# Loading the first two blocks of x as halves over two DMA queues, with the identity between them, and one sum of squares moved to VectorE

## The chip, the cores and the metric

The kernel runs on one core of one Trainium2 chip. A core has five engines with an instruction stream each: PE (TensorE, matrix products), ACT (ScalarE), DVE (VectorE), POOL (GpSimd) and SP (SyncE). SP and ACT each issue DMA transfers on a queue of their own: the profile calls SP's queue q1 and ACT's q10. The metric is the time of one execution on the device in microseconds. Before the change, three executions took 1043.51, 1043.86 and 1046.29 us; their median is 1043.86 us.

## What is computed

A decoder layer on 512 tokens of width 1024: a root-mean-square norm, one wide projection, three mixers, a gated merge, a feed-forward block and a last norm. The change touches the first lines only:

```python
def rmsnorm(x, g):
    xf = x.astype(jnp.float32)
    y = xf * lax.rsqrt(jnp.mean(xf * xf, axis=-1, keepdims=True) + NORM_EPS)
    return (y * g.astype(jnp.float32)).astype(x.dtype)
...
    for i in range(DEPTH):
        u = rmsnorm(x, ln1_g[i])
        proj = u @ w_in[i]
```

All that follows (attention, pooling, state-space scan, feed-forward) reads `proj`, so nothing of it can begin before the first tokens are normed and turned.

## The kernel before, in words

The 512 tokens are four blocks of 128. A block is loaded as two tiles of 128 x 512 floats (256 KB each): `xin[tb, 0]` and `xin[tb, 1]`, the left and the right half of the features. `load_x` (L1410 to L1413) issues the two transfers of one block. Before the change, block 0 goes out on SP's queue and block 1 on ACT's; then ACT's queue takes the 128 x 128 identity `eye` (L1418) and the norm's gains `g8` (L1419). SP's queue goes on with the first weight tile in two halves of 512 KB (`fetch(weights[0], 2)`, L179), the second of 1 MB, then blocks 2 and 3 of x and small tables.

ACT then loads a table (L1422), and PE runs `warm_up` (L1427), products of ones that no result depends on.

The opening loop (`for tb in range(2)`, around L1488 to L1500) takes blocks 0 and 1. For each it sums squares of both halves (`squares`: ACT at L432, DVE at L434; the accumulated sum is read by a short second instruction), forms the mean square `v` (L1492, L1493) and its root `sq` on ACT (L1494), refines the reciprocal on DVE (`r`, `rt`, L1495 to L1497), and multiplies the identity by it into a diagonal tile `diag[tb]` (L1498). A product of a block of x with `diag[tb]` turns the block and scales it at once: `turn_scale` (L1486), eight for a block, 16 PE instructions in the profile. The eight of block 0 are issued inside the loop, right behind `diag[0]`. Behind the loop PE turns `g8` (L1502, with the identity), then takes the eight of block 1.

On ACT, behind the loop, stand two casts of the first weight tile (`wh`, L191), then the eight evacuations `turned` (L1456, high part `uh`, with the low part `ul` on DVE at L1457), then two casts of the second weight tile, sums of squares for blocks 2 and 3 (`row_squares`), and their scaling (L1523 on ACT, L1521 on DVE). POOL forms the low part of the first weight tile (L211). PE goes on with `begin` (L1469): 80 instructions on the first 256 tokens, then the transposes of the scaled blocks 2 and 3 (L1534), then the rest.

The order on PE, ACT, DVE and POOL is that of the program text (`manual_schedule` over these four engines); SP follows the order in which its transfers are asked for. An engine executes in order: an instruction that waits holds back all behind it.

Of the kernel before, what the change touches and what calls it, by code (L numbers as in the profile page):

```python
# [16 lines left out]
P = 128  # L17
S = 512
# [65 lines left out]
def trunk(ctx: ExitStack, tc, out, x, rel_bias, ln1_g, w_in, b_gate, w_a, pool_w, pool_scale, w_b,  # L84
# [3 lines left out]
    act, dve, pool, pe, sp = nc.scalar, nc.vector, nc.gpsimd, nc.tensor, nc.sync  # L88

    x, w_in, w_a, w_b, w_c, w_o = x[0], w_in[0], w_a[0], w_b[0], w_c[0], w_o[0]  # L90
# [17 lines left out]
    def T(name, dt=F32, shape=(P, S)):  # L108
        return big.tile(list(shape), dt, name=name, tag="t")
# [7 lines left out]
    def small(name, shape, dt=F32):  # L117
        return tiny.tile(list(shape), dt, name=name, tag="tiny")
# [310 lines left out]
    def squares(eng, src, ss):  # L429
        junk = T("junk")  # L430
        if eng is act:
            act.activation(junk, src, AF.Square, accum_out=ss)  # L432
        else:
            dve.scalar_tensor_tensor(junk, src, 1.0, src, OP.mult, OP.mult, accum_out=ss)  # L434
# [972 lines left out]

    xin, warm = {}, small("warm", [P, 1])

    def load_x(tb, eng=sp):  # L1410
        for h in range(2):
            t = xin[tb, h] = T("xin")
            eng.dma_start(t, x[tb * P:(tb + 1) * P, h * S:(h + 1) * S])  # L1413

    g8, g1 = T("g8"), cpool.tile([P, KD], F32, name="g1")
    load_x(0)
    load_x(1, act)
    act.dma_start(eye, c_eye)  # L1418
    act.dma_start(g8[:KD, :P], ln1_g[0].rearrange("(k p) -> k p", p=P))  # L1419
    dve.memset(ones, 1.0)  # L1420
    dve.memset(warm, 1.0)
# [7 lines left out]
    fetch(weights[0], 2)  # L1429
    fetch(weights[1])  # L1430
    load_x(2)
    load_x(3)
    sp.dma_start(ramp, c_ramp.partition_broadcast(P))
# [51 lines left out]
    def turn_scale(tb, k):  # L1485
        pe.matmul(bank(k)[:, tb * P:(tb + 1) * P], x_block(tb, k), diag[tb][:, :P], start=True, stop=True)  # L1486

    for tb in range(2):  # L1488
        s0, s1, v, sq, r, rt = (small(n, [P, 1]) for n in ("s0", "s1", "v", "sq", "r", "rt"))
        squares(act, xin[tb, 0], s0)  # L1490
        squares((dve, act)[tb], xin[tb, 1], s1)
        dve.tensor_scalar(v, s0, 1.0 / D, EPS, OP.mult, OP.add)  # L1492
        dve.scalar_tensor_tensor(v, s1, 1.0 / D, v, OP.mult, OP.add)  # L1493
        act.activation(sq, v, AF.Sqrt)  # L1494
        dve.reciprocal(r, sq)  # L1495
        dve.scalar_tensor_tensor(rt, r, v, r, OP.mult, OP.mult)
        dve.tensor_scalar(rt, rt, -0.5, 1.5, OP.mult, OP.add)  # L1497
        dve.tensor_scalar(diag[tb][:, :P], eye, r, rt, OP.mult, OP.mult)  # L1498
        if tb == 0:
            for k in range(KD):  # L1500
                turn_scale(0, k)
# [15 lines left out]
    for tb in (2, 3):  # L1517
        for h in range(2):
            t = xin[tb, h]
# [98 lines left out]
```

## Time and profile before

| what | value |
|---|---|
| three executions, median | 1043.86 us |
| the profiled execution's own time | 1044.67 us |
| its span (first to last instruction in the records) | 1042.3 us |
| mean granted PE clock | 0.997 |
| PE busy | 1030.8 us |
| DVE busy | 689.9 us |
| ACT busy | 483.7 us |
| POOL busy | 136.1 us |
| bytes moved by DMA | 115.51 MB |

The profiled execution took 1044.67 us, 2.37 us more than its span, and 0.81 us more than the median of the three. In the views below, a row of the timeline gives its start, its length, engine, line and operation, and in brackets what the engine waited for; `x8` says that eight instructions are merged into the row. A row with `SPq` or `ACTq` is the issue of a transfer by that engine, not the transfer. A row of the chain of waits gives start, length, and what the program's end hung on in that stretch. A row of the stages gives each engine's busy time, then the granted clock of PE, the share of the DMA engines and GB/s. A row of the DMA queues gives packets, MB, and the packets' time as a share of 16 engines.

### The profile page before, as it was taken

What the parts mean: (1) busy time and instruction counts of PE and PEld (TensorE: products, weight loads), DVE (VectorE), ACT (ScalarE), POOL (GpSimd) and SP (SyncE); (2) the same over time, 40 slices, a digit from 0 to 9 for tenths busy, and PEclk for the clock granted to TensorE, in tenths of its full rate; (3) what the DMA queues carried; (4) which work ended last, traced back from release to release, by engine and by line L of the source; (5) the groups of instructions that cost most, each with busy time, mean ns of one, the idle gap of its engine ahead of it and who ended that gap; (6) DMA issues with size and microseconds to landing.
All of it is one profiled execution on the core that took longest, in us unless ns stands there. A gap on an engine that the chain in (4) does not pass through costs nothing.

```text
span 1042.3 us, 13073 instructions
## 1 busy us (share of the span) xinstructions
PE 1030.8 (99%) x5196; PEld 859.8 (82%) x5196; DVE 689.9 (66%) x924; ACT 483.7 (46%) x779; POOL 136.1 (13%) x118
## 2 busy tenths in 40 slices
PE   8999999999999999999999999999999999999997
PEld 8988877898888887787887888898888888888885
DVE  4563565774356647576568855767778769876776
ACT  5432445443474263566554333544445544454332
POOL 1680000000000001100134500001111000111002
PEclk9999999999999999999999999999999999999999
DMA  8445222027222354541243535443222232412222
GB/s 268 132 111 153 91 72 75 31 56 205 83 81 81 81 154 109 152 123 50 81 139 106 196 118 202 165 141 120 83 93 70 81 122 83 160 41 81 81 81 81
DMA packets 116427, 115.51 MB, mean 111 GB/s; under 512 B 5235, under 2 KB 101302, under 8 KB 116367
## 3 DMA queue, kind: packets, MB, share of 16 engines
q1 hardware_dynamic: 115775, 113.83, 35.8%
q8 instruction: 41, 0.67, 0.3%
q10 hardware_dynamic: 592, 0.86, 0.2%
q14 instruction: 19, 0.16, 0.0%
HBM read 110.87 MB, written 2.22 MB: 109 GB/s over the span
## 4 chain that ended last, share of the span: by engine, by line
PE 94%; DVE 3%; DMA 1%; ACT 1%; issue 1%; POOL 0%; ACTq 0%; DVEq 0%; POOLq 0%
PE pa L230 32%; PE pu L230 22%; PE pb L230 12%; PE pqk L230 9%; PE pd L230 7%; PE pa L1469 2%; PE ps L656 1%; PE pu L1279 1%; PE po L695 1%; PE pt L683 1%; PE ppw L230 1%; PE py L955 1%; DVE wl L211 1%; PE pyo L961 1%; DMA wb<-wd 1%; DMA eye<-in_c_eye_dram 1%
## 5 line engine op out<-in xcount | busy, mean ns | idle before, releaser
L211 DVE TENSOR_TENSOR wl<-raw,wh 128x2048 fp32r<-128x2048 f32 (+3 forms) x92 | 214.5, 2332 | 52.1 <-ACT wh L191 43.9
L191 ACT CAST wh<-raw 128x1024 fp32r<-128x1024 f32 (+3 forms) x182 | 183.6, 1026 | 42.4 <-DMA raw<-in_w_in_dram 15.2
L230 PE MATMUL pa<-uh,wh 128*128 128x512 f32 x384 | 98.7, 399 | 0.0
L1152 DVE SCALAR_TENSOR_TENSOR hc<-pu,fcol,hc 128x510 f32<-128x510 f32 x88 | 65.9, 748 | 48.8 <-ACT hc L1149 47.2
L230 PE MATMUL pa<-uh,wl 128*128 128x512 f32 x384 | 95.0, 389 | 0.8 <-DVE wl L211 0.8
L230 PE MATMUL pa<-ul,wh 128*128 128x512 f32 x384 | 95.0, 389 | 0.0
L230 PEld LDWEIGHTS pa<-uh,wl 128*128 128x128 f32 x384 | 72.0, 188 | 16.2 <-DVE wl L211 1.3
L230 PEld LDWEIGHTS pa<-ul,wh 128*128 128x128 f32 x384 | 72.1, 188 | 15.2
L230 PE MATMUL pu<-uh,wh 128*128 128x512 f32 (+1 forms) x352 | 83.6, 379 | 0.0
L230 PE MATMUL pu<-ul,wh 128*128 128x512 f32 (+1 forms) x352 | 83.5, 379 | 0.0
L230 PE MATMUL pu<-uh,wl 128*128 128x512 f32 (+1 forms) x352 | 83.5, 379 | 0.0
L230 PEld LDWEIGHTS pa<-uh,wh 128*128 128x128 f32 x384 | 70.2, 188 | 15.3 <-issue 1.0
L230 PEld LDWEIGHTS pu<-ul,wh 128*128 128x128 f32 x352 | 64.2, 188 | 12.5
L230 PEld LDWEIGHTS pu<-uh,wl 128*128 128x128 f32 x352 | 64.2, 188 | 12.5
L230 PEld LDWEIGHTS pu<-uh,wh 128*128 128x128 f32 x352 | 64.1, 188 | 12.4
L1157 POOL TENSOR_TENSOR hc<-hc 128x512 f32<-128x512 f32 x22 | 31.7, 1441 | 288.4 <-DVE hc L1152 253.6
L1149 ACT ACTIVATE hc<-pu,fcol,fcol 128x512 f32<-128x512 f32 x40 | 31.2, 779 | 80.5 <-PE pu L230 80.5
L934 POOL TENSOR_TENSOR xd<-xc,dec 128x512 f32<-128x512 f32 x6 | 6.4, 1063 | 360.0 <-DVE xc L925 334.3
L677 ACT ACTIVATE sb<-sb,nm 128x128 f32<-128x128 f32 (+1 forms) x72 | 30.1, 419 | 24.1 <-DVE nm L674 17.2
L1050 ACT ACTIVATE sg<-pa,col 128x512 f32<-128x512 f32 x24 | 16.5, 687 | 50.8 <-PE pa L230 50.7
L230 PE MATMUL pqk<-uh,wh 128*128 128x512 f32 x144 | 36.9, 393 | 0.0
L230 PE MATMUL pqk<-ul,wh 128*128 128x512 f32 x144 | 36.3, 389 | 0.0
(347 smaller groups left out, 1818.1 us busy)
## 6 DMA issues: line engine op xcount, KB each, us to landing
raw<-in_w_in_dram SPq DMA_DIRECT2D x25, 1024.0 KB
raw<-in_ffn_w_up_dram SPq DMA_DIRECT2D x22, 1024.0 KB
raw<-in_w_in_dram SPq DMA_DIRECT2D x20, 512.0 KB
raw<-in_w_o_dram SPq DMA_DIRECT2D x8, 1024.0 KB
raw<-in_ffn_w_down_dram SPq DMA_DIRECT2D x6, 1024.0 KB
raw<-in_w_b_dram SPq DMA_DIRECT2D x4, 1024.0 KB
al<-ad SPq DMA_DIRECT2D x16, 256.0 KB
w<-in_ffn_w_down_dram SPq DMA_DIRECT2D x4, 1024.0 KB
```

The lines of the kernel that those rows point to most:

```text
L191: act.copy(job.high[:, :, o], job.raw[:, :, o])
L211: (eng or dve).tensor_tensor(l[:, :, o], job.raw[:, :, o], h[:, :, o].bitcast(F32), OP.subtract)
L230: pe.matmul(ps, l, r, start=first and n == 0, stop=last and n == total - 1)
L656: pe.matmul(pss[i][:, o:o + w * P], q[r, n * P:(n + 1) * P], k[r, kb * P:(kb + w) * P], start=True, stop=True)
L677: act.activation(sb[:, off:off + w * P], sb[:, off:off + w * P], AF.Exp, bias=nm[:, n, h:h + 1], accum_out=ls[:, n, h:h + 1])
L683: pe.transpose(pt[:, o:o + P], sb[:, o:o + P], eye)
L695: pe.matmul(po[DH * hh:DH * hh + DH, n * P:(n + 1) * P], V[g, kb + i][:, (2 * c + hh) * DH:(2 * c + hh + 1) * DH], probs[2 * c + hh, nb][: ...
L1050: act.activation(s, ps, AF.Sigmoid, bias=col[:, o:o + 1])
L1149: act.activation(t, ps, AF.Identity, bias=ff["c1"][:, ff["b"] + m:ff["b"] + m + 1], scale=fw(2, m))
L1152: dve.scalar_tensor_tensor(t[:, sh:], ps[:, :S - sh], fw(k, m), t[:, sh:], OP.mult, OP.add)
L1157: pool.tensor_tensor(a, a, t, OP.mult)
L1469: pe.matmul(first[2 * n + j][:, lo:hi], a[:, k, j * P:(j + 1) * P], b[:, k, lo:hi], start=a is wh and b is uh and k == 0, stop=a is wl and ...
```

## The change

Three edits, all in the opening. `load_x` takes a pair of queues, one for each half. The two halves of block 0 go out on SP's and ACT's queue, so do the halves of block 1, and the identity stands between them on ACT's queue. The squares of the right half of block 1 are summed on DVE, where ACT did it.

The order on the two queues is:

| | SP's queue | ACT's queue |
|---|---|---|
| before | block 0 left, block 0 right, weights 0 ... | block 1 left, block 1 right, identity, `g8` |
| after | block 0 left, block 1 left, weights 0 ... | block 0 right, identity, block 1 right, `g8` |

```diff
@@ -1407,15 +1407,15 @@
-    def load_x(tb, eng=sp):
+    def load_x(tb, engs=(sp, sp)):
         for h in range(2):
             t = xin[tb, h] = T("xin")
-            eng.dma_start(t, x[tb * P:(tb + 1) * P, h * S:(h + 1) * S])
+            engs[h].dma_start(t, x[tb * P:(tb + 1) * P, h * S:(h + 1) * S])
 
     g8, g1 = T("g8"), cpool.tile([P, KD], F32, name="g1")
-    load_x(0)
-    load_x(1, act)
+    load_x(0, (sp, act))
     act.dma_start(eye, c_eye)
+    load_x(1, (sp, act))
     act.dma_start(g8[:KD, :P], ln1_g[0].rearrange("(k p) -> k p", p=P))
@@ -1488,7 +1488,7 @@
     for tb in range(2):
         s0, s1, v, sq, r, rt = (small(n, [P, 1]) for n in ("s0", "s1", "v", "sq", "r", "rt"))
         squares(act, xin[tb, 0], s0)
-        squares((dve, act)[tb], xin[tb, 1], s1)
+        squares(dve, xin[tb, 1], s1)
         dve.tensor_scalar(v, s0, 1.0 / D, EPS, OP.mult, OP.add)
```

## The prediction

> **What bounds the kernel now.** I read the page's chain of waits first, then the same chain in order of time, then the timeline of the opening.
>
> ```profile
> span 1042.3 us, 13073 instructions
> PE 94%; DVE 3%; DMA 1%; ACT 1%; issue 1%; POOL 0%; ACTq 0%; DVEq 0%; POOLq 0%
> ```
>
> ```profile
> 1.66 6.35 DMA eye<-in_c_eye_dram
> 8.11 0.34 DVE diag L1498
> 8.53 2.85 PE uT L1486 x16
> 11.38 0.20 PE pa L1502
> 11.59 2.66 PE uT L1486 x16
> 14.24 9.60 PE pa L1469 x80
> 23.84 1.75 PE uT L1534 x16
> ```
>
> The kernel is PE from end to end, except that the chain begins with the identity's transfer. What the change can win is therefore the start of PE's useful work and its pace up to the first long run of products. The identity, third on ACT's queue, lands at 1.66 + 6.35 = 8.01 us, and the first `diag` follows at 8.11. The identity alone is late by little, as the timeline shows:
>
> ```profile
> 0.74 0.89 ACTq L1413 DMA_DIRECT2D xin<-in_x_dram  x2
> 0.74 0.87 SPq L1413 DMA_DIRECT2D xin<-in_x_dram  x2
> 1.05 5.35 PE L1427 MATMUL pa<-ones 128*128 128x128 f32 x24 [1.05 <-DVE relb L511]
> ...
> 4.73 0.63 ACT L432 ACTIVATE junk<-xin 128x512 f32<-128x512 f32 x1 [0.34 <-DMA xin<-in_x_dram]
> 5.26 0.19 ACT L432 ACTIVATION_READ_ACCUMULATOR junk<-xin 128x1 f32 x1
> 5.70 0.69 DVE L434 SCALAR_TENSOR_TENSOR junk<-xin 128x512 f32<-128x512 f32 x1 [4.67 <-DMA xin<-in_x_dram]
> ...
> 6.32 0.15 DVE L1492 TENSOR_SCALAR v<-s 128x1 f32<-128x1 f32 x1
> 6.69 0.20 ACT L1494 ACTIVATE sq<-v 128x1 f32<-128x1 f32 x1 [1.24 <-DVE v L1493]
> 6.80 0.61 ACT L432 ACTIVATE junk<-xin 128x512 f32<-128x512 f32 x1
> 7.38 0.15 DVE L1497 TENSOR_SCALAR rt<-rt 128x1 f32<-128x1 f32 x1
> 7.41 0.61 ACT L432 ACTIVATE junk<-xin 128x512 f32<-128x512 f32 x1
> 8.11 0.34 DVE L1498 TENSOR_SCALAR diag<-eye,r,rt 128x128 f32<-128x128 f32 x1 [0.58 <-DMA eye<-in_c_eye_dram]
> 8.82 0.20 ACT L1494 ACTIVATE sq<-v 128x1 f32<-128x1 f32 x1 [0.70 <-DVE v L1493]
> 8.93 2.09 ACT L191 CAST wh<-raw 128x1024 fp32r<-128x1024 f32 x2
> 9.70 0.35 DVE L1498 TENSOR_SCALAR diag<-eye,r,rt 128x128 f32<-128x128 f32 x1
> 12.78 3.44 ACT L1456 ACTIVATE uh<-uT,g 128x256 fp32r<-128x256 f32 x8 [1.76 <-PE uT L1486]
> ```
>
> The scale of block 0 is ready at 7.38 + 0.15 = 7.53, so 0.58 us of DVE's wait is the identity's. Behind it stands a second late transfer: the right half of block 0, for which DVE waits until 5.70, while ACT began the left half at 4.73. And PE stands still from the warm-up's end (6.40) to 8.51, for which it pays twice:
>
> ```profile
> 6.40:8.51 2.11, 0.00 (x1) 0.00 (x0) 1.16 (x7) 1.43 (x5) 0.00 (x0) 1.00 1.21 295
> ...
> 9.50:13.00 3.50, 3.50 (x18) 3.25 (x17) 0.67 (x3) 1.73 (x3) 2.96 (x2) 0.51 1.08 355
> ```
>
> For the 3.50 us that begin 1.0 us after the gap the granted clock is 0.51: 3.50 x 0.49 = 1.7 us of PE work lost, in the turns of blocks 0 and 1. The two groups of turns with `g8` between them take 8.53 to 14.24 = 5.71 us; at full clock they would take 4.0, about 1.9 a group and 0.2 for `g8`.
>
> **The change part by part.** ACT issues four transfers before its table load in both kernels, and SP two ahead of the weights; the issue rows keep their count and place, so the issuing itself costs nothing new. What moves is which bytes stand ahead of which.
>
> *Block 0.* The queues' packets tell when each transfer ran.
>
> ```profile
> q1 hardware_dynamic: 150, 0.28, 50.0%
> q10 hardware_dynamic: 137, 0.25, 34.7%
> ```
>
> ```profile
> DMA packets 272, 0.47 MB, mean 315 GB/s; under 512 B 23, under 2 KB 47, under 8 KB 272
> ```
>
> From 1.75 to 3.75 us (first pair of rows) each queue moved one half block of 0.26 MB side by side. ACT's first place now holds block 0's right half, so it should land with the left one, near 4.7. From 3.75 to 5.25 (third row) 0.47 MB went at 315 GB/s.
>
> DVE then sums from 4.75 on, until 4.75 + 0.69 = 5.44. ACT's sum of the left half is read at 5.26 + 0.19 = 5.45, and this becomes the bound: `v` at about 5.5 instead of 6.32. From `v` to the scale's end takes 7.53 - 6.32 = 1.21, so the scale is ready at 6.7. The identity, now second on ACT's queue, runs beside block 1's left half: 0.07 + 0.26 = 0.33 MB at 315 GB/s is 1.05 us from 3.75, so its last packet falls by 4.8. How long from the last packet to the landing, the identity of before tells:
>
> ```profile
> q10 hardware_dynamic: 197, 0.13, 20.5%
> ...
> q10 hardware_dynamic: 2, 0.00, 0.1%
> ```
>
> In 5.25 to 7.25 ACT's queue still moved 197 packets, after 7.25 two; the landing is at 8.01, so 0.76 later. The identity then lands near 5.6, over 1 us before it is needed. `diag[0]` starts at 6.75 and PE at 7.15 instead of 8.51: 1.36 us earlier. PE's gap shrinks from 2.11 to 0.75 us.
>
> *The clock.* The trace shows no gap of 0.75 us at the start, so this is bounded: with the half-clock stretch gone 1.7 us come on top, with the stretch as before nothing. I take it as gone, being nearer to the long busy stretches at 1.00 than to a gap of 2.11. Every other wait of PE until 14.24 then counts as well.
>
> The Trainium skill (TensorE: Matmul & The Clock Gate, Why this matters for your kernels) says that the clock falls for PE gaps longer than about 3 us. The row above disagrees: 2.11 us were followed by 0.51. By the page the gap did not cause the stretch, and the change would leave it; that is the first of the rivals.
>
> *Block 1.* The left half, on SP's queue by 4.8, lands near 5.6; ACT squares it behind its root of block 0, at about 6.0. The cost is in the right half, third on ACT's queue and beside the first weights on SP's. How ACT's queue fares against those weights, the identity of before shows, from 5.75 to 7.0:
>
> ```profile
> q1 hardware_dynamic: 692, 0.35, 101.2%
> q10 hardware_dynamic: 129, 0.06, 16.4%
> ```
>
> One packet of ACT's against 5.4 of the weights', in 1.25 us. The right half is 128 packets of 2 KB: by packets it takes 128 x (2 KB + 5.4 x 0.5 KB) = 0.62 MB at (0.35 + 0.06) MB / 1.25 us = 1.9 us, from about 4.8, so it ends at 6.7 and lands at 7.5. The bounds: one packet against one weight packet, 0.33 MB or 1.0 us, landing at 6.6; or the same bytes a microsecond as the identity, 0.06 / 1.25, 5.4 us, landing at 11.0. The row is nearer to packets, since two streams of equal packets did not share equally there by bytes either; I take 7.5.
>
> DVE is free at 6.75 + 0.34 = 7.1 and so waits 0.4 us for it; behind it on DVE stand only block 1's chain and the copy of the gains. From this sum's start to the scale's end took 5.70 to 7.53 = 1.83 for block 0, so `diag[1]` starts at 9.35 (before: 9.70) and PE's second group at 9.75. PE finishes its first group at 7.15 + 1.9 = 9.05 and `g8` at 9.3: 0.45 us idle. The second group ends at 11.7, against 14.24: 2.5 us.
>
> *What ACT does with it.* ACT loses one sum (0.61 + 0.19 for reading). Its root of block 1 comes at 7.5 + (6.69 - 5.70) = 8.5 instead of 8.82, so the first cast could start at 8.6. The second cast needs the second half of the first weights:
>
> ```profile
> q1 hardware_dynamic: 2066, 1.06, 102.5%
> ```
>
> From 5.0 to 9.0 SP's queue moved 1.06 MB, which is this tile of 1.05 MB; landing at 9.0 + 0.76 = 9.75. The bytes ahead of it are the same in both kernels. So the second cast runs from 9.75 to 10.8 (2.09 / 2 each) instead of ending at 11.02, and `turned` starts at 10.85, instead of 12.78 behind PE's slow turns: ACT and all behind it on ACT is 1.9 us earlier, PE 2.5. What is late next is the scaling of blocks 2 and 3, of which ACT's part ended at 22.12 + 1.34 = 23.46 and PE's first weight load of them began at 23.57:
>
> ```profile
> 22.12 1.34 ACT L1523 ACTIVATE xin<-xin,r 128x512 f32<-128x512 f32 x2 [1.08 <-DVE r L426]
> ...
> 23.57 0.46 PEld L1534 LDWEIGHTS uT<-eye,xin 128*128 128x128 f32 x4
> ```
>
> 0.1 us of slack. PE, 2.5 us early, meets scaled blocks that are 1.9 us early and waits the 0.5 us between: **the sum is 1.9 + 0.1 = 2.0 us**, less 0.1 for small waits: 1.9. After that the chain is PE, and where it leaves PE it starts from PE's progress, so the shift carries to the end: 1044.67 - 1.9 = 1042.8 for the profiled execution, and by the median, 0.81 lower, **1042.0**.
>
> **The rivals.** *The clock stretch stays* (or the timed executions of before did not have it). PE's second group then runs from 9.75 at half clock until 13.0 and the rest at full: 1.6 us of its 1.9 are done by then, it ends at 13.3, and 14.24 - 13.3 = 0.9 us is left: 1043.86 - 0.9 = 1043.0 (this and the next times go from the median). For it: there is still a gap in the same place, and one more of 0.45. Against it: together they are 1.2 us, not 2.11. The clock page of the Trainium skill (TensorE: Matmul & The Clock Gate) is on this rival's side, as said above.
>
> *Only the identity counts.* If block 0's right half is no sooner on the other queue, the scale stays at 7.53 and only the wait of 0.58 goes; with the stretch at half clock as before the gain is 0.6: 1043.3. For it: the two queues together moved 315 GB/s already, so a second queue adds no rate. Against it: half as many bytes stand ahead of that half as before. The Trainium skill (DMA: Bandwidth & Descriptors, Rules for kernel authors) says that spreading DMAs over issuing engines brings no bandwidth and only saves issue time; the rows above agree as to the rate, and by that rule alone the time would be this rival's 1043.3; the forecast goes by the order of the bytes instead.
>
> *The right half of block 1 starves, and the kernel is slower.* On ACT's queue beside the weights it may get bytes as the identity did, landing at 11.0. ACT's second cast ends 0.99 + 2.2 = 3.2 us behind the start of DVE's sum; `turned` is later than 12.78 once the half lands after 9.5. At 11.0 it starts at 14.25: 1.5 us lost, and PE, idle from 9.3 to 13.3, falls to half clock again and loses up to 1.7 more: 1.5 to 3.2 us, 1045.4 to 1047.1. For it: ACT's queue moved only 0.06 MB in 1.25 us there. Against it: equal packets in number, not in bytes, explain that as well.
>
> *The order does not reach the queues*, or the shift is lost in a later wait: 1043.9. Against it: the transfers are issued in program order in the rows above.
>
> **How the numbers follow.** The forecast (1.5 to 2.3 us gained) has 0.52, the clock stretch staying 0.20, the identity alone 0.08, starvation 0.12, no effect 0.08. The forecast's own range is 1041.5 to 1042.4; the executions of before spread over 2.8 us, so a median moves by some 0.7 us by itself. The range for the time is 1040.7 to 1044.4: it takes in the first two rivals and no effect, and leaves out most of starvation. A change of under 0.3% (3.1 us) can hardly be told from none here. To be faster by that, the time must be under 1040.7, which the sum reaches only with luck in the median: 0.10. Slower by that needs the worst of starvation: 0.05. The rest, 0.85, is no change.
>
> **What would show it.** In the profile after: DVE's first sum of squares near 4.7 and not 5.7; `diag[0]` near 6.75 with no wait for the identity; PE's turns from 7.15 with the granted clock at 1.00 until 14; DVE waiting for block 1's right half until about 7.5; the casts of the first weights ending at 10.8; `turned` at 10.85; the products of L1469 from 11.7; and a short wait of PE at L1534, near 21.6, for ACT's scaling. A landing of block 1's right half after 9.5 makes the prediction wrong in sign, a half-clock stretch behind 9.5 halves it.

## The result, and the profile after

The changed kernel took 1042.30 us in the median of 22 executions (1041.21 to 1043.84), the kernel before 1043.68 us in 22 executions beside them (1041.24 to 1046.29). The ratio is 0.9987 with a 95% interval of 0.9981 to 0.9993: 1.4 us or 0.13% faster. The interval leaves out 1, and the gain is well inside the 0.3% that the prediction named as the bound of "no change". The forecast was 1042.0 us. One profiled execution in the experiments (the first set with the longer warm-up) took 1475.71 us at a mean granted clock of 0.65; it is left out, and that kernel was profiled again.

The changed kernel's page and its chain of waits in order of time (start, length, what the end hung on):

```profile
span 1038.6 us, 13072 instructions
PE 97%; DMA 1%; DVE 1%; ACT 0%; issue 0%; ACTq 0%; DVEq 0%; SPq 0%
```

```profile
1.66 5.62 DMA xin<-in_x_dram
7.31 0.70 DVE junk L434 x2
...
9.18 0.36 DVE diag L1498
9.54 0.04 issue
9.58 2.05 PE uT L1486 x16
11.63 9.68 PE pa L1469 x80
21.31 1.75 PE uT L1534 x16
```

The chain no longer begins with the identity but with a half block of x, block 1's right one, and goes through its sum and `diag[1]` to PE's second group of turns. The run of 80 products starts at 11.63 instead of 14.24, the turns of blocks 2 and 3 at 21.31 instead of 23.84: the opening is 2.5 us shorter in this pair of profiles. The same stretch in the timeline of the changed kernel (start, length, engine, line, and what the engine waited for):

```profile
4.61 0.63 ACT L432 ACTIVATE junk<-xin 128x512 f32<-128x512 f32 x1 [0.23 <-DMA xin<-in_x_dram]
4.79 0.69 DVE L434 SCALAR_TENSOR_TENSOR junk<-xin 128x512 f32<-128x512 f32 x1 [3.76 <-DMA xin<-in_x_dram]
...
6.66 0.34 DVE L1498 TENSOR_SCALAR diag<-eye,r,rt 128x128 f32<-128x128 f32 x1
...
7.06 2.05 PE L1486 MATMUL uT<-diag,xin 128*128 128x128 f32 x16 [1.50 <-DVE diag L1498]
7.31 0.69 DVE L434 SCALAR_TENSOR_TENSOR junk<-xin 128x512 f32<-128x512 f32 x1 [0.30 <-DMA xin<-in_x_dram]
...
9.85 1.04 ACT L191 CAST wh<-raw 128x1024 fp32r<-128x1024 f32 x1 [0.41 <-DMA raw<-in_w_in_dram]
...
10.80 3.02 ACT L1456 ACTIVATE uh<-uT,g 128x256 fp32r<-128x256 f32 x8
```

Block 0's right half is there at 4.79, not at 5.70; `diag[0]` follows at 6.66 with no wait for the identity. PE's turns start at 7.06, after a gap of 1.50 us and not of 2.11. And the clock holds. In this row of the stages the column before the last two is the granted clock:

```profile
9.50:13.00 3.50, 3.42 (x29) 3.40 (x30) 1.79 (x7) 3.15 (x8) 3.48 (x2) 1.00 1.08 356
```

The same 3.50 us had 0.51 before and 18 PE products where there are 29 now. How much of the gain that is, and whether it was the transfers that brought it, the experiments tell.

### The profile page after: what moved, and what is told of

It is laid out like the page before. It is cut to its first block, busy times and chain, and to the rows that moved or that the text cites. A ratio compares the mean times of both kernels' runs of the same rounds, so it can differ in the third digit from the quotient of the medians.

```text
span 1038.6 us, 13072 instructions
## 1 busy us (share of the span) xinstructions
PE 1028.1 (99%) x5196; PEld 857.8 (83%) x5196; DVE 689.4 (66%) x926; ACT 482.9 (46%) x777; POOL 135.8 (13%) x118
## 4 chain that ended last, share of the span: by engine, by line
PE 97%; DMA 1%; DVE 1%; ACT 0%; issue 0%; ACTq 0%; DVEq 0%; SPq 0%
PE pa L230 36%; PE pu L230 22%; PE pb L230 12%; PE pqk L230 9%; PE pd L230 7%; PE pa L1469 2%; PE ps L656 1%; PE pu L1279 1%; PE po L695 1%; PE pt L683 1%; PE ppw L230 1%; DMA al<-ad 1%; PE py L955 1%; DMA xin<-in_x_dram 1%; PE pyo L961 1%; PE pst L972 0%
## 5 line engine op out<-in xcount | busy, mean ns | idle before, releaser
L627 DVE COPY k<-pqk 128x512 f32<-128x512 f32 x9 | 6.2, 690 | 45.3 <-PE pqk L230 45.3
```

## The experiments

There were three sets, each timed beside the kernel before in five rounds on one chip. The first holds "before again", "sum on DVE alone", "identity first, alone" and "two queues alone"; the second "changed again", "changed, warm-up 17", "right half on SP" and "before, warm-up 20"; the third the rest. The kernel before had medians of 1043.84, 1043.15 and 1043.76 us in them. Ratios are to that kernel, with 95% intervals. They are not quotients of the medians: "changed, identity third" has 1042.44 against 1043.76 us, a quotient of 0.9987, and a ratio of 0.9993. "Gap" is PE's longest wait before a group of turns, "half clock" whether the profile shows a granted clock of 0.5 in the opening, "start" the start of the run of 80 products. These three and the span come from one profiled execution each.

| kernel | median us | ratio (interval) | gap us | half clock | start us | span us |
|---|---|---|---|---|---|---|
| before (as shown ahead) | 1043.68 | 1 | 2.1 | yes | 14.24 | 1042.3 |
| before again | 1043.75 | 0.9993 (0.9985 to 1.0002) | 2.6 | yes | 14.10 | 1041.5 |
| sum on DVE alone | 1044.10 | 1.0000 (0.9991 to 1.0008) | 2.2 | yes | 14.20 | 1041.8 |
| identity first, alone | 1042.39 | 0.9990 (0.9981 to 0.9999) | 1.5 | no | 12.69 | 1040.7 |
| two queues alone | 1042.01 | 0.9981 (0.9972 to 0.9989) | 0.9 | no | 11.88 | 1039.2 |
| changed | 1042.30 | 0.9987 (0.9981 to 0.9993) | 1.5 | no | 11.63 | 1038.6 |
| changed again | 1042.23 | 0.9988 (0.9979 to 0.9998) | 1.5 | no | 12.66 | 1040.6 |
| changed, warm-up 17 | 1042.45 | 0.9989 (0.9981 to 0.9998) | 0.6 | no | 11.82 | 1039.6 |
| changed, warm-up 6 | 1042.43 | 0.9993 (0.9984 to 1.0003) | 2.9 | yes | 12.73 | 1039.7 |
| changed, identity third | 1042.44 | 0.9993 (0.9983 to 1.0002) | 1.7 | no | 12.42 | 1039.9 |
| right half on SP | 1041.58 | 0.9986 (0.9977 to 0.9995) | 1.2 | no | 11.54 | 1039.0 |
| right half on SP, warm-up 17 | 1042.46 | 0.9994 (0.9985 to 1.0004) | none | no | 11.44 | 1039.7 |
| before, warm-up 20 | 1041.47 | 0.9981 (0.9971 to 0.9990) | - | - | - | - |
| before, warm-up 20, again | 1041.54 | 0.9984 (0.9975 to 0.9993) | 1.1 | no | 12.57 | 1039.7 |

**The kernel before, again.** No edit.

> The kernel before, unchanged. Theory (the clock is a matter of where its windows fall): the times spread over some 4 us as in the 22 runs (1041.2 to 1046.3) around 1043.7, ratio 1.000, and the profile may show the half-clock stretch behind 9.5 us at another place or not at all; the DVE and ACT stall near 530 to 568 us need not be there. Rival (both belong to the kernel): half clock from 9.5 to 13.0 and the chain off PE from 528 to 568 again.

The chain of waits and a row of the stages of this execution:

```profile
14.10 9.59 PE pa L1469 x80
```

```profile
8.40:11.70 3.30, 3.30 (x16) 3.30 (x16) 1.04 (x5) 2.18 (x3) 1.80 (x1) 0.51 1.12 332
```

Half the theory held. The half-clock stretch came at another place (8.4 to 11.7), so its position moves, but the profile showed it again, and again in the kernel with the sum alone. In all three profiles with the old transfers and the old warm-up it is there. The chain did not leave PE near 530 to 568 us this time, as the theory allowed.

The record has the mean granted clock of every execution, and this accounts for much of the spread of the times. A stretch of 3.4 us at half clock takes 0.0016 off that mean (3.4 x 0.5 / 1042), and half clock at the program's end (from 1040.37 us on in the first profile of the kernel before) takes another 0.001 to 0.002 off. So 0.997 or less is a sign of the stretch in the opening. It is not a proof: the profiled execution of the sum alone has the stretch and reads 0.998. The kernel before, sorted by this reading:

| set | at 0.998 or 0.999 | their median us | at 0.997 or less | their median us |
|---|---|---|---|---|
| first | 4 | 1042.28 | 29 | 1044.06 |
| second | 12 | 1042.34 | 21 | 1043.88 |
| third | 12 | 1041.50 | 23 | 1044.10 |

In the third set the two groups do not even touch: 1040.8 to 1042.3 us and 1043.5 to 1045.5. All 33 executions of the changed kernel read 0.998 or 0.999. In the second set it took 1042.23 us, about what the executions of the kernel before took that kept their clock (1042.34). As far as times can tell, then, most of the gain of the change is that the stretch no longer occurs.

**The two queues alone.** Block 1's right half is summed on ACT, as before.

```diff
-        squares(dve, xin[tb, 1], s1)
+        squares((dve, act)[tb], xin[tb, 1], s1)
```

> The two queues alone, block 1's right half summed on ACT again. Theory: the order of the bytes makes the gain and the move of the sum next to none, since the second cast waits for the weights' second half (9.85) in any case: DVE's first sum at 4.8, PE's turns from 7.1, second group 0.1 to 0.2 us later than in the changed kernel, products from 11.6 to 11.8; time 1042.3 to 1042.5. Rival (the sum on DVE is needed): ACT, with 0.8 us more in front of the casts, is late and the gain over before falls to half, 1043.0.

```profile
7.61 0.63 ACT L432 ACTIVATE junk<-xin 128x512 f32<-128x512 f32 x1 [1.17 <-DMA xin<-in_x_dram]
...
8.66 2.16 ACT L191 CAST wh<-raw 128x1024 fp32r<-128x1024 f32 x2
```

1042.01 us, a little under the expected range, with DVE's first sum at 4.62, turns from 6.90 and products from 11.88. The theory held in its direction: the move of the sum is worth nothing that can be seen here. Its reason did not hold: the two casts follow each other (2.16 us for both), with no wait for weights worth naming. ACT had stood idle for 1.17 us when the right half landed, so the sum cost nothing there, and the chain goes, as in the changed kernel, from that landing through the sum and `diag[1]` to PE's second group.

**The sum on DVE alone.**

```diff
-        squares((dve, act)[tb], xin[tb, 1], s1)
+        squares(dve, xin[tb, 1], s1)
```

> The sum on DVE alone, queues as before. Theory: no gain; DVE takes the sum up behind diag[0] (8.45), diag[1] comes at about 10.4 instead of 9.7, the casts end at 11.5 instead of 11.0; 0 to 0.4 us slower than before where PE is at full clock, nothing where it is at half clock: 1043.7 to 1044.1. Rival: it makes part of the gain, 1043.0 or less.

The ratio is 1.0000 (0.9991 to 1.0008), the median 1044.10 us; `diag[1]` started at 10.20 instead of 9.70. As the theory expected, no gain.

**The identity first, alone.** Both halves of block 0 on SP's queue, both of block 1 on ACT's, the identity ahead of them.

```diff
     load_x(0)
+    act.dma_start(eye, c_eye)
     load_x(1, act)
-    act.dma_start(eye, c_eye)
```

> The identity first on ACT's queue, ahead of block 1, block 0 on SP's queue as before. Theory: only DVE's wait of 0.58 us goes, diag[0] at 7.55 and PE's turns from 7.95; gain 0.4 to 0.9 us: 1042.8 to 1043.3. Rival (the identity was all that counted): the whole gain, 1042.3, with the turns from 7.1.

1042.39 us, with a ratio (0.9990) that cannot be told from the changed kernel's (0.9987). Who waited for whom on PE (total, times, longest), a row of the stages, and the chain:

```profile
PE uT L1486 <- DVE v L1492: 1.5, 1, 1.5
```

```profile
8.10:13.00 4.90, 4.52 (x37) 4.31 (x38) 2.21 (x9) 4.36 (x9) 2.42 (x2) 1.00 1.12 337
```

```profile
12.69 9.59 PE pa L1469 x80
```

Mechanically the theory was right: only DVE's wait went, and the turns started at 8.05, 0.46 us earlier than before. But in this execution that shortened the gap from 2.1 to 1.5 us (0.14 of it because the warm-up ended at 6.54 and not at 6.40), and the clock stayed at 1.00. The run of 80 starts 1.5 us earlier, not 0.5: the size came from the clock, and neither side of the expectation had that.

The clock did not stay in every execution. Five of the 11 read 0.996 or 0.997, with a median of 1043.04 us; the other six, the profiled one among them, have 1041.93. So the identity's place alone keeps the clock only at times, where the changed kernel kept it in all 33.

**The kernel before with a longer warm-up**, in two sets. Every transfer and every instruction of the opening is as before; PE multiplies ones until 7.3 us.

```diff
-WARM = 12
+WARM = 20
```

> The kernel before with 20 products of warm-up instead of 12, so that PE is busy until about 8.4. Theory (the gap of 2.1 us lets the clock fall): no half-clock stretch, the turns of block 0 still from 8.5 at full clock, products from 12.5 to 13.0 instead of 14.2; the times' spread shrinks to about that of the changed kernel (1041.2 to 1043.8) and the median falls by 0.5 to 1.0: 1042.7 to 1043.2. Rival (the stretch has nothing to do with the gap): the same spread and 1043.7 or slightly more.

> The kernel before with 20 products of warm-up, a second time, for a profile at an undisturbed clock. Theory (the change's gain is for the most part the clock, which falls in a gap of 2.1 us or more): turns of block 0 from about 8.5, full clock throughout, first products' run of 80 from 12.7 to 12.9, time 1041.3 to 1041.8, as good as the changed kernel or better with none of its edits. Rival (its time came from something later): half clock in the opening, or a start of the 80 at 14, and the gain behind it.

1041.47 and 1041.54 us, ratios of 0.9981 and 0.9984. The second set's waits, stages and chain:

```profile
PE uT L1486 <- DVE v L1492: 1.1, 1, 1.1
```

```profile
8.40:13.00 4.60, 4.60 (x38) 4.46 (x39) 2.44 (x9) 3.92 (x8) 3.10 (x2) 1.00 1.11 344
```

```profile
8.40 2.04 PE uT L1486 x16
10.43 0.15 PE pa L1502
10.59 1.98 PE uT L1486 x16
12.57 9.60 PE pa L1469 x80
```

The turns start at 8.40, as in the second profile of the kernel before (8.53 in the first), and the identity is as late as there; yet both groups run at full clock (2.0 us each), and the products start 1.5 to 1.7 us earlier than in those two profiles. This is the clock's share by itself. The times lie under the range of the first expectation, which had priced the clock at 0.5 to 1.0 us, and in that of the second. One constant brings at least as much as the change of the transfers; the intervals overlap, so more cannot be claimed.

**The changed kernel with a shorter warm-up.** The transfers of the change, but PE idle from 4 us on.

```diff
-WARM = 12
+WARM = 6
```

> The changed kernel with 6 products of warm-up instead of 12: the same transfers, the same start of the turns near 7, but PE idle from about 3.7 on. Theory (clock): the turns and the first products run at half clock for 3.4 us or more, the 80 products start at 12.5 to 14 instead of 11.6 to 12.7, time 1043.3 to 1044.2: the whole gain of the change is lost although every transfer is as early as in it. Rival (the earlier start of the turns is what gains): 1042.3 to 1042.6.

The waits, the stages and the chain:

```profile
PE uT L1486 <- DVE diag L1498: 3.1, 2, 2.9
```

```profile
9.00:10.00 1.00, 0.90 (x5) 0.58 (x3) 0.86 (x5) 0.94 (x2) 0.00 (x0) 0.50 1.13 327
```

```profile
12.73 9.59 PE pa L1469 x80
```

The clock fell as the theory says, and the start lies in the expected range. The time did not: 1042.43 us where 1043.3 to 1044.2 were expected, ratio 0.9993 (0.9984 to 1.0003). By the interval the gain is no longer shown, but it is not shown to be lost either. The start says more: with the stretch in both, the products begin at 12.73 here and at 14.10 to 14.24 with the old transfers. So in the opening the earlier turns are worth 1.4 us where the clock falls. Where it holds, the old transfers start the products at 12.57 (the longer warm-up) and the new ones at 11.63 to 12.66, which is 0.9 us earlier or not at all. That the whole gain of this kernel would be lost with the clock is too strong. The mean clock does not sort the times here: three executions, the profiled one among them, read 0.996 and took 1041.92 to 1042.28 us, the nine at 0.998 or 0.999 took 1042.03 to 1044.48. Why is open.

**The changed kernel with a longer warm-up.**

```diff
-WARM = 12
+WARM = 17
```

> The changed kernel with 17 products of warm-up, which closes its gap of 0.7 to 1.5 us. Theory: the changed kernel keeps its clock as it is, so nothing is gained: 1042.2 to 1042.5; in executions where the warm-up runs long at half clock it delays the turns by up to 0.5. Rival (the smaller gap still costs the clock at times): up to 0.5 less, 1041.8, and a narrower spread.

1042.45 us, products from 11.82. No gain, as the theory said: the changed kernel, with gaps of 1.5 us in its profiles, has no clock to win back.

**The changed kernel again.** No edit.

> The changed kernel, unchanged. Theory: 1042.3 with a spread of some 2.6 us, profile at full clock from 6 us on, products from 11.6. Whether the chain leaves PE near 530 to 568 us tells if that stall comes and goes by itself. Rival: half clock at times here too.

1042.23 us. Its timeline and two rows of its chain:

```profile
8.34 0.69 DVE L434 SCALAR_TENSOR_TENSOR junk<-xin 128x512 f32<-128x512 f32 x1 [1.50 <-DMA xin<-in_x_dram]
```

```profile
12.66 9.60 PE pa L1469 x80
...
537.10 5.96 DMA wb<-wd
```

Full clock, but block 1's right half came at 8.34 where the first profile had 7.31, and the products started 1.0 us later for it. And the chain leaves PE near 530 to 568 us, through a transfer `wd` to `wb` and a row of DVE work. It did so in the first profile of the kernel before and not in its second, and it did not in the first profile of the changed kernel: each kernel shows both, so that detour comes and goes and is not the change's.

**Both halves of block 1 on SP's queue**, none behind the weights, then the same with a longer warm-up.

```diff
-    load_x(1, (sp, act))
+    load_x(1, (sp, sp))
```

> The changed kernel with both halves of block 1 on SP's queue behind block 0's left half; ACT's queue has block 0's right half, the identity and g8. Theory: the right half lands near 6.3 instead of 7.3, DVE takes it up at 7.05, diag[1] at 8.9 instead of 9.2, PE's second group 0.25 us earlier; the weights' second half lands as before or up to 0.1 later, so ACT gains nothing and PE then waits at its first products or at the scaled blocks: 0 to 0.25 us faster, 1042.1 to 1042.3. Rival (the wait for the right half sets the end): the full 0.3 us and no wait behind it.

```diff
-WARM = 12
+WARM = 17
```

> Both halves of block 1 on SP's queue (the identity second on ACT's) and 17 products of warm-up: PE without a gap, no half block behind the weights. Theory: the start of the 80 products is held at 11.5 by the cast of the weights' second half; 1041.2 to 1041.6 with a narrow spread. Rival (the warm-up runs over, or the opening no longer sets the end): 1041.9 or more.

Without the longer warm-up, the timeline and PE's waits read:

```profile
8.79 0.35 DVE L1498 TENSOR_SCALAR diag<-eye,r,rt 128x128 f32<-128x128 f32 x1
...
10.07 1.05 ACT L191 CAST wh<-raw 128x1024 fp32r<-128x1024 f32 x1 [0.73 <-DMA raw<-in_w_in_dram]
```

```profile
PE pa L1469 <- ACT uh L1456: 0.3, 1, 0.3
```

`diag[1]` is earlier by 0.4 us, ACT waits 0.73 us for the weights' second half, and PE then 0.3 us for ACT: what the theory said would be late next. 1041.58 us, under the expected 1042.1 to 1042.3, but the interval of its ratio (0.9977 to 0.9995) covers the changed kernel's 0.9988 in the same set: not shown to be faster. With the warm-up on top the products start earliest of all, at 11.44, and yet the time is 1042.46 us: the forecast of 1041.2 to 1041.6 failed. Its profile shows the same detour near 530 to 568 us as the first profile of the kernel before, and its way from the start of the 80 products to the end, 1028.2 us, is the longest of all profiles (1027.4 without the longer warm-up). Why 11 executions of it show none of the faster times is not settled.

**The identity third**, behind both right halves on ACT's queue.

```diff
-    act.dma_start(eye, c_eye)
     load_x(1, (sp, act))
+    act.dma_start(eye, c_eye)
```

> The changed kernel with the identity behind block 1's right half on ACT's queue, instead of between the two halves. Theory (what stands third on ACT's queue lands beside the weights): block 1's right half lands near 5.8 and the identity near 7.5 to 8, diag[0] at that time and not at 6.6; PE's gap is again 1.9 to 2.4 us and the half clock may return: 1042.5 to 1043.7. Rival (the place on the queue does not matter): as the changed kernel, 1042.3.

```profile
7.83 0.35 DVE L1498 TENSOR_SCALAR diag<-eye,r,rt 128x128 f32<-128x128 f32 x1 [1.25 <-DMA eye<-in_c_eye_dram]
```

The identity lands just ahead of 7.83, nearly as late as in the kernel before (8.11), where two half blocks stood ahead of it on the same queue as they do here. The third place, beside the weights, is the late one, for the 64 KB tile as for the 256 KB one of the changed kernel (7.31 to 8.34). The gap was 1.69 us and not the expected 1.9 to 2.4, and in the profiled execution the clock held. In others it did not: four of the 12 read 0.996 or 0.997, and they are the four slowest, 1043.22 to 1044.69 us; the other eight took 1041.67 to 1042.49. The median, 1042.44 us, is just under the expected 1042.5 to 1043.7.

## Why the prediction was right, point by point

*What moved, and to where.* Right, within 0.2 us in the profiled execution: turns at 7.06 (forecast 7.15), block 1's right half at 7.31 (7.5), `diag[1]` at 9.18 (9.35), second group at 9.58 (9.75), second cast ending at 10.89 (10.8), `turned` from 10.80 (10.85), products from 11.63 (11.7). That it fits so closely is in part chance: in the second profile of the changed kernel the right half came at 8.34, `diag[1]` at 10.21 and the products at 12.66.

*How the right half fares beside the weights.* By packets, as chosen. The queues of the changed kernel from 5.75 to 7.0 us:

```profile
q1 hardware_dynamic: 491, 0.25, 68.7%
q10 hardware_dynamic: 122, 0.19, 42.1%
```

One packet of ACT's against 4.0 of the weights' (5.4 for the identity before), and 0.19 MB in the time in which the identity's queue had moved 0.06. The starvation rival is refuted in its size. What it named is real: the landing varied from 7.31 to 8.34 us between the two profiles of the changed kernel, and with it the start.

*The clock.* Taken as restored, and it was, in all 33 executions of the changed kernel by their mean clock. The kernel before with the longer warm-up shows its share by itself, 1.5 to 1.7 us of the start. But the step that led there was weaker than it looked. The gap was forecast at 0.75 us and was 1.50: the warm-up ended at 5.56 us (1.05 + 4.51) and not at 6.40. So the change left a gap nearer to the 2.11 of before than to none, and the choice "taken as gone" was right with some luck. The end of the twelve products moves with the moment at which the clock rises to full: it lies between 5.56 and 6.54 us in the profiles.

In every profile at hand, gaps of 2.1, 2.2, 2.6 and 2.9 us are followed by half clock, gaps of 1.7 us and less are not. The Trainium skill (TensorE: Matmul & The Clock Gate, Why this matters for your kernels) puts the limit at gaps above about 3 us; the four gaps named were shorter and lost the clock, so here the measurement decides. The Trainium skill (TensorE: Matmul & The Clock Gate, Part 1) says that the monitor works in free-running windows of about 3.4 us; the stretches of 3.4 us that begin at different times in different executions agree with it.

*The rival "only the identity counts"* is where the prediction failed. It gave 0.6 us to the identity's earlier landing "with the stretch at half clock as before". The step was to take the clock in that case as unchanged: the shorter gap kept it in six of 11 executions, and the identity alone gave 1042.39 us. The forecast therefore credited the second queue with much that a shorter gap brings by any means. What the second queue adds is that the gap is short enough each time.

*What is late next.* "PE waits the 0.5 us between" did not happen. ACT's part of the scaled blocks:

```profile
19.73 1.34 ACT L1523 ACTIVATE xin<-xin,r 128x512 f32<-128x512 f32 x2 [1.08 <-DVE r L426]
```

It ended at 21.07, 2.4 us earlier and not 1.9: the eight `turned` took 3.02 us, where the 3.44 of before contained waits for PE's slow turns. The opening's gain in the profile was 2.5 us and not 2.0.

*The sum.* 1.9 us was forecast, 1.4 measured, with an interval of 0.7 to 2.0. The one profile pair had 2.5 in the opening, the other pair (14.10 to 12.66) 1.4. For the profiled execution the forecast was 1042.8 us, and it took 1041.21: 3.5 us less than before, of which the opening is 2.5. The way from the start of the 80 products to the end of the span took 1028.1 us before and 1027.0 after, and 1027.0 to 1028.2 over the thirteen profiles, so the rest of that difference cannot be put down to the change. The median gained less than the opening of the first pair. The forecast took the clock's 1.7 us off the median as if every execution of the kernel before had lost them, but 28 of the 101 in the three sets read 0.998 or 0.999. That the median came within 0.3 us of the forecast is thus partly luck: a term too large for the median stood beside one too small for the opening.

## What to carry to other kernels

When PE's first useful work starts behind a warm-up, look for the gap between the two and for the granted clock behind it, before working on the transfers: a gap of 2.1 us was followed by a loss of 1.7 us of PE work here, and eight more products of ones won at least as much as a new order of the loads. An early transfer is worth what ends last behind it; of three edits here one (the sum) was worth nothing that could be seen, and one (the identity's place) kept the clock by itself in about half of the executions. With gains of 1 to 2 us in 1043, repeat the profile: two profiles of one kernel differed by 1.0 us in the opening and by a detour of the chain later on. And sort the executions by their mean granted clock before comparing medians, as far as it sorts the times (with the short warm-up it did not).

## What the runs showed of the hardware that was not expected

The granted clock in the profile's rows reads 1.00 from the start, but the products say otherwise. Groups by line of the kernel before, first the warm-up (0 to 7 us), then turns just ahead of the stretch (9.2 to 9.5 us) and inside it (10 to 11 us); the last number but one is the mean in ns:

```profile
L1427 PE MATMUL pa<-ones 128*128 128x128 f32 x24 | 5.4, 421 | 1.1 <-DVE relb L511 1.1
...
L1486 PE MATMUL uT<-diag,xin 128*128 128x128 f32 x5 | 0.7, 275 | 0.0
...
L1486 PE MATMUL uT<-diag,xin 128*128 128x128 f32 x7 | 1.7, 421 | 0.0
```

The warm-up's products took 421 ns, the duration at half clock, so PE was at half clock for most of the warm-up, where the row says 1.00. Before the first recorded change the column cannot be relied on; the duration of equal products can. In the changed kernel's profile the warm-up's products took 428 ns until 4.2 us and 275 ns from 4.6 us on; there the clock rose earlier, and so the warm-up ended earlier.

The traces also keep the moments at which the granted clock changes, and these say more than the length of the gap. The last two columns give PE's idle time in the 3.41 us behind the first change to full clock, and what came next:

| profile | first change to full, us | idle in the next 3.41 us | then |
|---|---|---|---|
| before | 6.13 | 2.11 | half clock, 9.55 to 12.96 |
| before again | 4.78 | 2.44 | half clock, 8.20 to 11.61 |
| sum on DVE alone | 5.86 | 2.20 | half clock, 9.28 to 12.69 |
| changed, warm-up 6 | 4.54 | 2.33 | half clock, 7.95 to 11.36 |
| changed | 4.37 | 1.50 | full |
| identity first, alone | 6.88 | 1.21 | full |
| changed, identity third | 7.23 | 1.00 | full |

In the six other undisturbed profiles the idle time is 1.22 us or less, and the clock stays full. Each half-clock stretch begins 3.41 us behind the first change and lasts as long. So what counted here was how much of the gap fell into one such piece of 3.41 us: between 1.50 and 2.11 us of it lies the limit, as far as the openings show. With the identity third the gap was 1.69 us, but only 1.00 of it lay in the piece. That also fits a kernel that loses its clock in some executions and not in others, since the moment of the first change differs from one to the next (4.18 to 7.23 us in these profiles); the executions without a profile cannot show it.
